# A hybrid attention, recurrence and expert layer on one core: expert weights in 8 KB rows, fetched token rows, and three smaller moves

## The chip, the cores and the metric

The program runs on one core of a Trainium2 chip. A core has TensorE (PE in the profile; its weight loads are PEld), VectorE (DVE), ScalarE (ACT), GpSimd (POOL), SyncE (SP, which here only requests transfers) and 16 DMA engines between HBM and the core's own memory, which has 128 partitions. The metric is the device time of one execution in microseconds, lower is better.

## The reference

Shapes: 512 tokens of latent stream, 256 of context, width 1024, 16 experts of hidden width 1024, float32 throughout.

```python
def block(x, ctx, c, c_ctx, w):
    sh1, sc1, g1, sh2, sc2, g2 = modulation(c, w.ada_w, w.ada_b)      # silu(c) @ ada_w + ada_b
    h     = rmsnorm(x, n1) * (1 + sc1) + sh1
    a     = hgrn_both_directions(h, ctx)                               # gated linear recurrence, 8 heads
    b     = conv3(h)                                                   # short gated depthwise convolution
    o     = attend(h, ctx)                                             # 16 query heads, 4 key heads, head 64
    y     = sig(ga) * (a @ w_pa) + sig(gb) * (b @ w_pb) + sig(gc) * (o @ w_pc)
    x1    = x + g1 * (y @ w_out)
    return rmsnorm(x1 + g2 * experts(rmsnorm(x1, n2) * (1 + sc2) + sh2), fng)

def experts(h, router_w, w_gate, w_up, w_down):        # expert choice: each expert takes 64 of 512 tokens
    aff = softmax(h @ router_w)                        # 512 x 16
    w_sel, idx = top_k(aff.T, 64)
    xs  = h[idx]                                       # 16 x 64 x 1024
    hid = silu(xs @ w_gate) * (xs @ w_up)
    ys  = hid @ w_down * w_sel
    return zeros(512, 1024).at[idx].add(ys)
```

## The kernel before

The stages follow one another. Times are those of the profile's span: recurrence heads and the dense projections to about 540 us, attention to 806, the branch projections with their sigmoid gates to 1130, the output projection with the router's logits to 1190, the choice of tokens to 1215, eight expert pairs to 1661, and a tail to 1697.

**Large products in three passes.** A dense product is made as three passes over split operands (`hH,wh`, `hL,wh`, `hH,wl`, lines L185 to L187): each weight block of 1 MB or 0.5 MB arrives as `raw`, ACT copies it to `wh` (L90) and DVE takes the rest, `wl` (L91). So a block that has landed is of use to PE only when ACT, then DVE, have been over it.

**Attention.** 64 units (query head and quarter of the queries). A unit makes scores (L617, L618, tile `sc`), takes a row maximum on DVE, exponentials on ACT (L623, tile `e`), turns them by six PE transposes (L632, tile `tp`), evicts them half on ACT (L636, tile `pt`) and half on DVE, and multiplies with the values (L647). Scores run two units ahead. Between units a `Filler` issues steps of other dense products (the queries of the next key group, convolution, gate columns), in equal shares per unit. The queries of each group are normalised by a square root on ACT (L582), once for each of two halves; ACT's tables of square root and exponential exclude each other, so each use in the midst of exponentials costs two table loads. Turns of keys and queries (L562, L599) are issued in runs inside those filler steps.

**Branches.** For each of four column blocks, `wblock` requests the gate columns of `w_in`, then two slabs of `ada_w` (`ada_more`, 1 MB each, DVE multiplies each into `acc`, L742), then the projection block `w_p`. When a group of eight slabs is done, `column` turns its sums into a column over partitions: for each of 8 pieces one PE product of a 128x128 piece of `acc` with a single column of ones (L725).

**Experts.** Two experts are worked at a time, 64 tokens each, one in each half of the 128 columns of the stationary operand. Each pair streams 24 weight blocks of 1 MB (gate and up in 4 chunks of 256 channels, then down in 4) through SP's queue, L962, into a ring of 20 slots, plus four slots that hold the first blocks once. `refill` requests a block for each slot that was read. The first 24 requests stand in SP's queue behind the last weights of the output projection, so they go out while that product and the routing run. PE's order in this stage is the order of the code, not a scheduler's: gate and up of pair p (L1099, tiles `pg`, `pu`), then the gather of pair p+1 (L1048: tokens are picked by a product of `x1` with a scaled one-hot matrix `ohs`, 64 PE instructions, evicted by DVE L1053 and ACT L1051 into `xT`), the weights of the chosen tokens (L1062), the scatter of pair p-1 (L1085, L1086, added to `moe` by DVE L1090), the transposes of the hidden values (L1153, after silu on ACT L1139 and the product on DVE L1140), the turned one-hot (L1073, `by_slot`), and down of pair p (L1099, tile `py`). The last pair's down weights are cut into column blocks (`LASTC`), which the tail works one by one, followed by the final norm.

A weight block's layout in `more()`:

```python
wsrc += [mat[e, kk*256:kk*256+256].rearrange("(a p) f -> p a f", p=128) for e in pair]
```

Partition p gets rows p and p+128 of the 256, each a row of 4 KB in HBM.

Of the kernel before, what the change touches and what calls it, by code (L numbers as in the profile page):

```python
# [22 lines left out]
D = 1024  # L23
# [28 lines left out]
def body(tc, x, ctx, cvec, ada_w, ada_b, ada_b0, n1g, n2g, hgn, convw, qg, kg, fng, w_in, w_pa, w_pb, w_pc, w_out,  # L52
# [21 lines left out]
    iota = const.tile([128, 64], F32, name="iota")  # L74
# [96 lines left out]
    last_w = []  # L171

# [372 lines left out]
    def queries(g, w):  # L545
# [10 lines left out]
        qsps[g] = []  # L556
# [8 lines left out]

        for half in range(2):
            p = ps.tile([128, 2, 256], F32, name="d")
            n = 0
            for i in range(2):
                for _ in tok_steps(w, 2 + 2 * half + i, p[:, i]):  # L570
                    yield 1
                    n += 1
                    if half and n % 4 == 0:
                        turn_keys(n // 4 - 1)
                        yield 0.5
            qf = at.tile([128, 2, 4, 64], F32, name="qf")
# [6 lines left out]
            dve.reciprocal(ssq, ssq)  # L583
            dve.tensor_mul(qf, qf, ssq[:, :, :, None].to_broadcast([128, 2, 4, 64]))
# [7 lines left out]
    def turn_queries(g):  # L592
        qst = at.tile([128, 4, S], F32R, name="qst", bufs=2)
        for half, qsp in enumerate(qsps.pop(g)):
            for hp in range(2):
                p = psc.tile([128, 4, 128], F32R, name="tp")
                for h2 in range(2):
                    for t in range(2):
                        pe.transpose(p[:, 2 * h2 + t], qsp[:, t, 2 * hp + h2], identr)  # L599
                act.activation(qst[:, 2 * hp:2 * hp + 2, half * 256:half * 256 + 256],  # L600
                               p.rearrange("p (h t) c -> p h (t c)", t=2).bitcast(F32), AF.Copy)
                yield 0.7
        qsts[g] = qst

    qsps = {}
# [60 lines left out]
    def mixed(c, turn):  # L666

        def steps(w):
            t = turn()
            n = 0  # L670
            for cost in c[1](w):
                yield cost
                n += 1
                if n % 3 == 0:
                    yield next(t, 0.0)
            yield from t
        return c[0], steps
# [3 lines left out]
    Filler([mm0, c2[0], turn0]).drain()  # L681
    fill_items = []
    for g, c in ((1, c2[1]), (2, c2[2]), (3, c3[0])):
        mm, turn = q_items(g)
        fill_items += [mm, mixed(c, turn[1])]
# [5 lines left out]
    with tc.manual_schedule(engines=MANUAL):  # L691
# [4 lines left out]
        for u in range(len(units)):  # L696
            core(turn_probs, u)
            if u + 2 < len(units):
                while units[u + 2][0] not in qsts:
                    fl.fill(1)  # L700
                core(scores, u + 2)
            fl.fill(share / 2)
            while owed:
                owed.pop()()
            if u % 4 == 0 and u:
                core(values, u - 1)
# [15 lines left out]
    def column(src, put):  # L722
        p = pl.tile([128, KC], F32, name="tp")
        for k in range(KC):
            pe.matmul(p[:, k:k + 1], src[:, k * 128:(k + 1) * 128], ones[:, 0:1], start=True, stop=True)  # L725
        put(p)

    def ada_more():
# [14 lines left out]
        if k == KC - 1:  # L743
            lo, hi = accs[g][:, 0:1024], accs[g][:, 1024:2048]
            if g == 1:
                later.append(lambda: gate_rows(lo))
                later.append(lambda: column(hi, lambda p: dve.tensor_copy(ab2[:, 1], p)))
            else:
                later.append(lambda: column(lo, lambda p: dve.scalar_tensor_tensor(ab2[:, 0], p, 1.0, vecs[:, 1],
                                                                                  op0=OP.add, op1=OP.mult)))  # L750
# [25 lines left out]
    def branch(b, w_p, get):  # L776
        hs = ls = None
        for j2 in range(4):
            wg = wblock(w_in, W_GATE + b * 1024 + j2 * 256)
            ada_more()  # L780
            ada_more()
# [8 lines left out]
            wp = wblock(w_p, j2 * 256)  # L790
            for i in range(2):
# [61 lines left out]
    aff = xp.tile([128, 4, NE], F32, name="aff")  # L853
# [17 lines left out]
    def partial_logits(j2, t):  # L871
        tp = pr_.tile([128, 2, 2, 128], F32, name="tp", bufs=2)
        for kk in range(2):
            for i in range(2):
                pe.transpose(tp[:, kk, i], x1[:, t + i, j2 * 256 + kk * 128:j2 * 256 + kk * 128 + 128], ident)
# [32 lines left out]
    dve.reciprocal(ss2, ss2)  # L908
    pl4 = pr_.tile([128, 4, NE], F32, name="tp", bufs=2)
# [22 lines left out]
    wsel = sm.tile([128, NE // 2], F32, name="wsel")  # L932
    slot = sm.tile([128, 4, NE], F32, name="slot")
# [8 lines left out]
    for pr in range(NE // 2):  # L942
        pair = (2 * pr, 2 * pr + 1)
        for kk in range(4):
            for mat in (w_gate, w_up):
                wsrc += [mat[e, kk * 256:kk * 256 + 256].rearrange("(a p) f -> p a f", p=128) for e in pair]
        if pr < NE // 2 - 1:
            for kk in range(4):
                wsrc += [w_down[e, kk * 256:kk * 256 + 256].rearrange("(a p) f -> p a f", p=128) for e in pair]
# [7 lines left out]
    def more(n):  # L957
        for src in wsrc[len(loaded):len(loaded) + n]:
# [3 lines left out]
            sp.dma_start(t, src)  # L962
            loaded.append(t)
# [60 lines left out]
    xs = {}  # L1024
    hot = {}

    def one_hot(pr):
# [6 lines left out]
                          iota[:, None, None, :].to_broadcast(shape), op=OP.is_equal)  # L1034
        ohs = ma.tile([128, 4, 2 * CAP], F32, name="ohs")
        dve.tensor_mul(ohs, ohf, ss2[:, :, None].to_broadcast([128, 4, 2 * CAP]))
        hot[pr] = oh, ohf, ohs

    def gather(pr, k0, p, on_act):

        ohs = hot[pr][2]
        if pr not in xs:
            xs[pr] = ma.tile([128, KC, 2 * CAP], F32, name="xT")
        xT = xs[pr]
        n = p.shape[1]
        for i in range(n):
            for t in range(4):
                pe.matmul(p[:, i], x1[:, t, (k0 + i) * 128:(k0 + i + 1) * 128], ohs[:, t], start=t == 0, stop=t == 3)  # L1048
        for k in range(k0, k0 + n):
            if on_act:  # L1050
# [248 lines left out]
```

## Time and profile before

| | |
|---|---|
| time, median of 3 runs | 1703.13 us (1701.49 to 1704.36) |
| the profiled execution | 1698.42 us, of which its span is 1696.6 us |
| PE busy | 1607.2 us (95% of the span) |
| VectorE, ScalarE, GpSimd busy | 767.9, 527.7, 150.7 us |
| moved by DMA | 305.52 MB, mean 180 GB/s over the span |

The span is the time from the first to the last instruction of the profiled execution. The rows further down are of that one execution.

### The profile page before, as it was taken

How to read it: one execution, taken by the hardware profiler on the slowest of the kernel's cores; microseconds unless marked ns; L12 is line 12 of the kernel's file. 1: busy time of each engine (PE TensorE's matmuls, PEld its weight loads, DVE VectorE, ACT ScalarE, POOL GpSimd, SP SyncE). 2: the span in 40 equal slices, each digit the busy share in tenths (PEclk: the TensorE clock that was granted, in tenths of full speed). 3: DMA queues.
4: the chain of work that ended last, by engine and by line, in shares of the span. 5: the costliest groups of instructions: out<-in, count | busy, mean ns of one | idle time of the engine just before them, and what ended most of it. 6: DMA issues, size and time to landing. Idle time of an engine off the chain costs nothing.

```text
span 1696.6 us, 23600 instructions
## 1 busy us (share of the span) xinstructions
PE 1607.2 (95%) x9896; PEld 1207.7 (71%) x9896; DVE 767.9 (45%) x1173; ACT 527.7 (31%) x934; POOL 150.7 (9%) x142
## 2 busy tenths in 40 slices
PE   6999999999998899899999999999799999999996
PEld 4889898988898788788788888889244344444444
DVE  6364655556545666655646524343411222122124
ACT  4433324334225656654323223233010010011004
POOL 0021212222000000000000100110000000000005
PEclk9999999999999999999999999999899999999998
DMA  9410211122222000100555622348789999999995
GB/s 294 118 41 25 63 38 50 38 75 70 80 80 75 26 25 26 44 33 26 182 191 178 209 85 75 124 148 349 315 320 402 382 409 409 409 409 409 409 395 167
DMA packets 166287, 305.52 MB, mean 180 GB/s; under 512 B 6562, under 2 KB 115618, under 8 KB 164130
## 3 DMA queue, kind: packets, MB, share of 16 engines
q1 hardware_dynamic: 162624, 301.66, 48.9%
q10 hardware_dynamic: 3556, 2.35, 0.4%
q8 instruction: 78, 1.28, 0.3%
q14 instruction: 29, 0.24, 0.0%
HBM read 301.89 MB, written 2.10 MB: 179 GB/s over the span
## 4 chain that ended last, share of the span: by engine, by line
PE 83%; DVE 9%; ACT 5%; issue 2%; POOL 0%; DMA 0%; ACTq 0%; SPq 0%; DVEq 0%; POOLq 0%
PE d L185 14%; PE d L187 14%; PE d L186 14%; PE pg L1099 6%; PE pu L1099 6%; PE py L1099 6%; PE py L1048 3%; PE lv L304 2%; PE tp L647 2%; PE tp L632 2%; DVE wl L91 1%; PE mi L333 1%; PE sc L617 1%; PE sc L618 1%; ACT wh L90 1%
## 5 line engine op out<-in xcount | busy, mean ns | idle before, releaser
L185 PE MATMUL d<-hH,wh 128*128 128x512 f32 x640 | 257.2, 402 | 0.0
L187 PE MATMUL d<-hH,wl 128*128 128x512 f32 x640 | 253.4, 396 | 0.0
L186 PE MATMUL d<-hL,wh 128*128 128x512 f32 x640 | 252.4, 394 | 0.0
L91 DVE TENSOR_TENSOR wl<-raw,wh 128x2048 fp32r<-128x2048 f32 (+1 forms) x78 | 157.8, 2022 | 192.0 <-ACT wh L90 191.8
L90 ACT ACTIVATE wh<-raw 128x2048 fp32r<-128x2048 f32 (+1 forms) x78 | 128.9, 1652 | 218.2 <-PE d L186 167.4
L187 PEld LDWEIGHTS d<-hH,wl 128*128 128x128 f32 x640 | 121.0, 189 | 24.9
L185 PEld LDWEIGHTS d<-hH,wh 128*128 128x128 f32 x640 | 120.8, 189 | 22.3 <-issue 1.6
L186 PEld LDWEIGHTS d<-hL,wh 128*128 128x128 f32 x640 | 121.1, 189 | 21.3 <-issue 0.2
L1099 PE MATMUL pg<-mw,xT 128*64 128x512 f32 x512 | 115.6, 593 | 2.0 <-DVE xT L1053 2.0
L1099 PE MATMUL pu<-mw,xT 128*64 128x512 f32 x512 | 115.3, 592 | 0.0
L1099 PE MATMUL py<-mw,hT 128*64 128x512 f32 x448 | 97.7, 594 | 0.1
L315 POOL TENSOR_TENSOR kk<-kk,tt 128x384 f32<-128x384 f32 x56 | 77.0, 1376 | 190.8 <-DVE tt L317 143.6
L1099 PEld LDWEIGHTS pu<-mw,xT 128*64 128x64 f32 x512 | 36.7, 137 | 73.1 <-issue 72.8
L1099 PEld LDWEIGHTS pg<-mw,xT 128*64 128x64 f32 x512 | 36.1, 137 | 72.2 <-issue 68.8
L185 PE MATMUL d<-wh,hH 128*128 128x256 f32 x288 | 84.1, 292 | 0.0
L187 PE MATMUL d<-wh,hL 128*128 128x256 f32 x288 | 81.7, 284 | 0.0
L186 PE MATMUL d<-wl,hH 128*128 128x256 f32 x288 | 81.6, 283 | 0.0
L1140 DVE TENSOR_TENSOR hid<-hid,pu 128x1024 f32<-128x1024 f32 x8 | 9.8, 1221 | 154.4 <-PE pu L1099 148.0
L187 PE MATMUL d<-brh,wl 128*128 128x512 f32 x192 | 75.6, 396 | 2.6 <-DVE wl L91 2.6
L185 PE MATMUL d<-brh,wh 128*128 128x512 f32 x192 | 75.8, 396 | 1.7 <-ACT wh L90 1.5
L186 PE MATMUL d<-brl,wh 128*128 128x512 f32 x192 | 75.7, 396 | 0.0
L1099 PEld LDWEIGHTS py<-mw,hT 128*64 128x64 f32 x448 | 31.5, 137 | 60.8 <-issue 59.7
(354 smaller groups left out, 2998.1 us busy)
## 6 DMA issues: line engine op xcount, KB each, us to landing
mw<-in_w_gate_dram SPq DMA_DIRECT2D x64, 1024.0 KB, 18.2
mw<-in_w_up_dram SPq DMA_DIRECT2D x64, 1024.0 KB, 18.5
mw<-in_w_down_dram SPq DMA_DIRECT2D x62, 1024.0 KB, 17.4
raw<-in_w_in_dram SPq DMA_DIRECT2D x38, 1024.0 KB, 5.1
raw<-in_ada_w_dram SPq DMA_DIRECT2D x16, 1024.0 KB, 4.9
raw<-in_w_in_dram SPq DMA_DIRECT2D x24, 512.0 KB, 3.8
adaw<-in_ada_w_dram SPq DMA_DIRECT2D x8, 512.0 KB, 8.5
raw<-in_ada_w_dram SPq DMA_DIRECT2D x8, 512.0 KB, 7.8
```

The costliest lines, as they stand in the source:

```text
L90: act.activation(hi, src, AF.Copy)
L91: dve.tensor_sub(lo, src, hi)
L185: pe.matmul(p, lh(k), rh(k), start=k == 0, stop=False)
L186: pe.matmul(p, lh(k), rl(k), start=False, stop=False)
L187: pe.matmul(p, ll(k), rh(k), start=False, stop=k == KC - 1)
L304: pe.matmul(p[:, c], kc[:, c * 128:(c + 1) * 128], q_mix, start=True, stop=True)
L315: pool.tensor_mul(kb[:, :, 1], kb[:, :, 1], tb[:, :, 0, 0:1].to_broadcast([128, n2, m]))
L333: pe.matmul(pv[:, i], kt[:, i], v[:, c], start=True, stop=True)
L632: pe.transpose(tp[:, t], e[:, (t0 + t) * 128:(t0 + t + 1) * 128], ident)
L647: pe.matmul(av[hh * 64:hh * 64 + 64, i], va[:, t, g * 64:g * 64 + 64], pts[hh][:, t], start=t == 0, stop=t == 5)
L1048: pe.matmul(p[:, i], x1[:, t, (k0 + i) * 128:(k0 + i + 1) * 128], ohs[:, t], start=t == 0, stop=t == 3)
L1099: pe.matmul(dst[64 * e:64 * e + 64, hf_], src[:, k, 64 * e:64 * e + 64], wt[e][:, k2, hf_ * 512:hf_ * 512 + 512], start=k == 0, stop=k == ...
```

## The change

1. **8 KB rows.** Gate, up and down blocks (not the last pair's down) are laid out so that partition p gets rows 2p and 2p+1 of the 256, which are 8 KB in one piece. The channel order on partitions thus becomes even, odd. Whatever meets those weights must follow: `every2` takes every second column of `x1`, of the fetched rows and of `hid` as the stationary operand of the products and transposes; the router's rows and the second norm's gain are permuted on the host.
2. **Fetched token rows.** `x1` is stored to HBM (`xd`, four transfers of 512 KB on SP's queue). For pairs 2 to 7 the gather products are gone. The product that finds the chosen tokens' weights gets two more columns, the token's number and its norm factor. GpSimd fetches the 128 rows of 4 KB by an indirect transfer, DVE scales them, and PE turns them by 8 transposes (`turn_rows`). Pairs 0 and 1 still pick by products. The scatter stands behind the transposes of the hidden values now.
3. **A line of turns.** In attention, turns of keys and queries go into a list, `aside`, and are taken one at a time between units. The square root of a query group is taken once for both halves.
4. **Sums by ones.** `column` makes two products of a 128x128 matrix of ones with 512 columns of `acc`, and DVE takes the diagonal by a product with `ident` and a sum over the free axis.
5. **Slabs behind.** The two `ada_w` slabs of a column block are requested behind the projection block `w_p`, not ahead of it.

```diff
@@ queries
+        aside.extend([lambda i=i: turn_keys(i) for i in range(4)])
...
-            ssq = at.tile([128, 2, 4], F32, name="ssq", bufs=2)
-            dve.tensor_reduce(ssq, sq, axis=AX.X, op=OP.add)
-            act.activation(ssq, ssq, AF.Sqrt, scale=1.0 / 64, bias=eps)
+            dve.tensor_reduce(ssq[:, half], sq, axis=AX.X, op=OP.add)
+        act.activation(ssq, ssq, AF.Sqrt, scale=1.0 / 64, bias=eps)
@@ units
-            while owed:
+            if owed:
                 owed.pop()()
+            elif aside:
+                aside.pop(0)()
+                fl.fill(1)
@@ column
-        for k in range(KC):
-            pe.matmul(p[:, k:k + 1], src[:, k * 128:(k + 1) * 128], ones[:, 0:1], start=True, stop=True)
+        for h in range(2):
+            p = ps.tile([128, 512], F32, name="d")
+            pe.matmul(p, ones, src[:, h * 512:(h + 1) * 512], start=True, stop=True)
...
+            dve.tensor_reduce(col[:, 4 * h:4 * h + 4], dg, axis=AX.X, op=OP.add)
@@ branch
             wg = wblock(w_in, W_GATE + b * 1024 + j2 * 256)
-            ada_more()
-            ada_more()
...
             wp = wblock(w_p, j2 * 256)
+            ada_more()
+            ada_more()
@@ experts
+    for t in range(4):
+        sp.dma_start(xd[t * 128:(t + 1) * 128], x1[:, t])
...
-                wsrc += [mat[e, kk * 256:kk * 256 + 256].rearrange("(a p) f -> p a f", p=128) for e in pair]
+                wsrc += [mat[e, kk * 256:kk * 256 + 256].rearrange("(p a) f -> p (a f)", p=128) for e in pair]
...
+    def fetch(pr):
+        xg = mb.tile([128, D], F32, name="hid")
+        pool.indirect_dma_start(xg, None, xd, bass.IndirectOffsetOnAxis(ap=which.pop(pr), axis=0))
+        dve.tensor_scalar(xg, xg, norm[:, pr:pr + 1], None, op0=OP.mult)
+    def turn_rows(pr):
...
+        for k in range(KC):
+            pe.transpose(p[:, k // 4, k % 4], every2(xg, k), ident)
...
+        if 0 < pr and not last:
+            turn_rows(pr + 1)
...
-            gather(pr + 1, 0, pn[:, 0], False)
-            gather(pr + 1, 4, pn[:, 1], True)
-            weights(pr)
-        if not last and waiting:
-            scatter(*waiting, 2, ...)
+        elif pr + 2 < NE // 2:
+            weights(pr + 2)
         hT = ...
+        if not last and waiting:
+            scatter(*waiting, 2, ...)
+        if 0 < pr < NE // 2 - 2:
+            fetch(pr + 2)
```

The line numbers of the changed kernel differ from those of before. Three places of its order follow.

SP's queue at the first branch, before: the slabs `in_ada_w` of a block stand ahead of its projection block `in_w_pc`.

```order
L734 DMA raw<-in_ada_w_dram 128x2048 x2
L176 DMA raw<-in_w_pc_dram 128x8x256
L176 DMA raw<-in_w_in_dram 128x8x256
L734 DMA raw<-in_ada_w_dram 128x2048 x2
L176 DMA raw<-in_w_pc_dram 128x8x256
```

The same place in the changed kernel (L764 is the slab, L181 the dense block).

```order
L181 DMA raw<-in_w_pc_dram 128x8x256
L764 DMA raw<-in_ada_w_dram 128x2048 x2
L181 DMA raw<-in_w_in_dram 128x8x256
L181 DMA raw<-in_w_pc_dram 128x8x256
L764 DMA raw<-in_ada_w_dram 128x2048 x2
```

The projection block has moved ahead of the two slabs in each of the eight column blocks that have slabs.

SP's queue where the experts' first 24 blocks are requested, before: behind the last block of the output projection, from the sixth to the last request.

```order
L962 DMA mw<-in_w_gate_dram 128x2x1024 x2
L962 DMA mw<-in_w_down_dram 128x2x1024
L962 DMA mw<-in_w_up_dram 128x2x1024 x2
L962 DMA mw<-in_w_gate_dram 128x2x1024 x2
L962 DMA mw<-in_w_up_dram 128x2x1024 x2
L962 DMA mw<-in_w_down_dram 128x2x1024 x7
```

The same place in the changed kernel, with the four stores of `x1`.

```order
L1001 DMA mw<-in_w_gate_dram 128x2048
L1001 DMA mw<-in_w_down_dram 128x2048
L941 DMA xd<-x_8639 128x1024 x2
L1001 DMA mw<-in_w_up_dram 128x2048
L941 DMA xd<-x_8639 128x1024 x2
L1001 DMA mw<-in_w_gate_dram 128x2048
L1001 DMA mw<-in_w_up_dram 128x2048
L1001 DMA mw<-in_w_gate_dram 128x2048 x2
L1001 DMA mw<-in_w_up_dram 128x2048 x2
L1001 DMA mw<-in_w_down_dram 128x2048 x7
```

The stores, which need the finished `x1`, stand behind the first ten blocks, and fourteen blocks stand behind the first of them.

PE's queue between gate and up of a middle pair and its down, before (the scatter's row and its partner stand once for eight).

```order
L1099 MATMUL pu<-mw,xT 64x512 x8
L1048 MATMUL py<-ohs,x_8645 128x128 x32
L1062 MATMUL d<-aff,oh 128x16 x4
L1085 MATMUL pg<-hT,ohT 128x512
L1086 MATMUL pg<-yL,ohT 128x512
...
L1153 MATMUL d<-ident,hid 128x128 x8
L1073 MATMUL d<-identr,oh 128x128 x4
L1099 MATMUL py<-mw,hT 64x512 x32
```

The same place in the changed kernel (L1112 turns fetched rows, L1124 finds weights and token numbers, L1226 turns the hidden values, L1151 scatters, L1139 is `by_slot`).

```order
L1165 MATMUL pu<-mw,xT 64x512 x8
L1112 MATMUL py<-ident,hid 128x128 x8
L1124 MATMUL d<-aff,oh 128x18 x4
L1226 MATMUL d<-ident,hid 128x128 x8
L1151 MATMUL pg<-hT,ohT 128x512
L1152 MATMUL pg<-yL,ohT 128x512
...
L1139 MATMUL d<-identr,oh 128x128 x4
L1165 MATMUL py<-mw,hT 64x512 x32
```

The gather's 32 products (64 PE instructions in a trace, since each runs as two) have become 8 transposes, and the transposes of the hidden values stand ahead of the scatter.

## Rows read from the trace of the kernel before

**Rows 1.** The page: PE's busy time, and the DMA engines' share in 40 slices.

```profile
PE 1607.2 (95%) x9896; PEld 1207.7 (71%) x9896; DVE 767.9 (45%) x1173; ACT 527.7 (31%) x934; POOL 150.7 (9%) x142
DMA  9410211122222000100555622348789999999995
```

**Rows 2.** The chain that ended last: share of the span by engine.

```profile
PE 83%; DVE 9%; ACT 5%; issue 2%; POOL 0%; DMA 0%; ACTq 0%; SPq 0%; DVEq 0%; POOLq 0%
```

**Rows 3.** Stretches of the expert stage: start:end, length, busy time per engine, PEclk, DMA share, GB/s.

```profile
1215.00:1277.00 62.00, 58.60 (x326) 28.48 (x328) 6.98 (x18) 5.17 (x9) 0.00 (x0) 1.00 0.81 312
1277.00:1334.00 57.00, 54.89 (x292) 25.77 (x290) 12.02 (x18) 5.63 (x11) 0.00 (x0) 1.00 0.97 384
1334.00:1392.00 58.00, 55.88 (x296) 26.04 (x294) 11.74 (x18) 5.44 (x10) 0.00 (x0) 1.00 1.03 409
...
1564.00:1622.00 58.00, 55.89 (x298) 26.04 (x294) 11.00 (x16) 5.44 (x10) 0.00 (x0) 1.00 1.03 409
```

**Rows 4.** Timeline of PE between up of one pair and its down: start, length, work.

```profile
1419.28 3.84 PE L1048 MATMUL py<-ohs,x 128*128 128x128 f32 x32
1424.57 3.84 PE L1048 MATMUL py<-ohs,x 128*128 128x128 f32 x32 [1.46 <-DVE xT L1053]
1428.25 0.96 PE L1062 MATMUL d<-aff,oh 128*128 128x16 f32 x8
...
1433.69 1.03 PE L1153 MATMUL d<-ident,hid 128*128 128x128 f32 x8
...
1435.43 13.95 PE L1099 MATMUL py<-mw,hT 128*64 128x512 f32 x64
```

**Rows 5.** Line L1099 (all expert products): one of three lines on its waits for weights.

```profile
  DMA mw<-in_w_down_dram: 0.3, 1
```

**Rows 6.** The last weight request, its time to landing; PE's last column block.

```profile
L962 SPq DMA_DIRECT2D mw<-in_w_down_dram x1: 1231/1231/1231, 1664.8 to 1664.8; - x1
...
DMA to landing us min/median/max: 6.5/6.5/6.5
...
1680.49 1.97 PE L1194 MATMUL pg<-mw,hT 128*64 128x128 f32 x32
```

**Rows 7.** Timeline of DVE and ACT in the same pair as group 4.

```profile
1419.49 1.22 DVE L1140 TENSOR_TENSOR hid<-hid,pu 128x1024 f32<-128x1024 f32 x1 [24.74 <-PE pu L1099]
...
1415.99 1.02 ACT L1139 ACTIVATE hid<-pg 128x1024 f32<-128x1024 f32 x1 [21.96 <-PE pg L1099]
```

**Rows 8.** Stretches in which slabs of `ada_w`, 8 KB rows, move alone.

```profile
862.00:864.50 2.50, 2.50 (x12) 2.06 (x11) 0.00 (x0) 0.00 (x0) 0.00 (x0) 1.00 0.85 344
894.00:896.50 2.50, 2.50 (x13) 2.07 (x12) 1.85 (x3) 1.78 (x3) 0.00 (x0) 1.00 0.87 354
```

**Rows 9.** The page: transfers of 512 KB of `x` on ACT's queue, us to landing.

```profile
xr<-in_x_dram ACTq DMA_DIRECT2D x4, 512.0 KB, 12.0
```

**Rows 10.** Timeline of PE: eight products whose moving operand alternates single elements, then pairs.

```profile
308.51 1.49 PE L304 MATMUL lv<-qq,kc 128*128 128x128 f32 x8
312.36 1.12 PE L304 MATMUL lv<-qq,kc 128*128 128x128 f32 x8
```

**Rows 11.** Attention: what PE waited for in 546 to 727 us; ACT's groups in 540 to 806.

```profile
PE tp L632 <- ACT pt L636: 11.5, 7, 3.1
...
L623 ACT ACT_TABLE_LOAD x7 | 9.0, 1283 | 4.4 <-DVE mx L621 4.4
L582 ACT ACT_TABLE_LOAD x6 | 7.7, 1283 | 0.1
```

**Rows 12.** Start of the first branch: DVE and PE in the timeline, and a stretch.

```profile
813.60 2.35 DVE L742 SCALAR_TENSOR_TENSOR acc<-raw,sc,acc 128x2048 f32<-128x2048 f32 x1
...
821.21 0.79 PE L187 MATMUL d<-brh,wl 128*128 128x512 f32 x1 [2.58 <-DVE wl L91]
...
819.90:826.70 6.80, 5.49 (x13) 4.33 (x14) 3.64 (x3) 1.91 (x1) 0.00 (x0) 0.50 0.52 176
```

**Rows 13.** PE's groups in 990 to 1130 us: the single-column products.

```profile
L725 PE MATMUL tp<-ones,acc 128*128 128x1 f32 x31 | 3.6, 250 | 0.0
```

More of the change, by code (lines that the diff above doesn't have):

```diff
@@ L571, in queries @@
                     yield 1
[L572 to L576, printed above, removed]
+            qf = at.tile([128, 2, 4, 64], F32, name="qf", bufs=2)
+            qfs.append(qf)
             act.activation(qf.rearrange("p t h d -> p t (h d)"), p, AF.Copy)
@@ L593, in turn_queries, with turn @@
         qst = at.tile([128, 4, S], F32R, name="qst", bufs=2)
[L594 to L605, printed above, removed]
+        def turn(half, hp):
+            p = psc.tile([128, 4, 128], F32R, name="tp")
+            for h2 in range(2):
+                for t in range(2):
+                    pe.transpose(p[:, 2 * h2 + t], qsps[g][half][:, t, 2 * hp + h2], identr)
+            act.activation(qst[:, 2 * hp:2 * hp + 2, half * 256:half * 256 + 256],
+                           p.rearrange("p (h t) c -> p h (t c)", t=2).bitcast(F32), AF.Copy)
+            if half and hp:
+                qsts[g] = qst
+        aside.extend([lambda i=i: turn(i // 2, i % 2) for i in range(4)])
+        return iter(())
+    qsps, aside = {}, []
     units = [(g, hp, qt, hh) for g in range(4) for hp in range(2) for qt in range(4) for hh in range(2)]
@@ L664, in q_items, with early_part, later_part @@
         return (W_AQ + g * 256, lambda w: queries(g, w)), (None, lambda: turn_queries(g))
[L666 to L677, printed above, removed]
+    parts = []
+    def early_part(c, w):
+        it = c[1](w)
+        parts.append(it)
+        for _ in range(KC):
+            yield next(it)
+    def later_part():
+        yield from parts.pop()
     c2, c3 = conv_items(2, at, "u", 1), conv_items(3, at, "u", 1)
     mm0, turn0 = q_items(0)
-    Filler([mm0, c2[0], turn0]).drain()
+    first = Filler([mm0, c2[0], turn0])
+    first.fill(33)
+    for _ in range(4):
+        first.fill(4)
+        aside.pop(0)()
+    first.drain()
+    for _ in range(4):
+        aside.pop(0)()
     fill_items = []
@@ L1023, in body @@
     pm, pm_e = opn("pm", space=PSUM, bufs=1)
-    xs = {}
-    hot = {}
+    xs, hot, which, fetched = {}, {}, {}, {}
     def one_hot(pr):
@@ L1103, in early @@
     def early(k0):
-        gather(0, k0, ps.tile([128, 2, 128], F32, name="d"), False)
+        pick(0, k0, ps.tile([128, 2, 128], F32, name="d"), False)
     with tc.manual_schedule(engines={mybir.EngineType.DVE}):
         one_hot(0)
+        scaled(0)
         early(0)
+    turned = {}
     waiting = None
@@ L1140, in body @@
         dve.tensor_mul(hid, hid, pu.rearrange("p a b -> p (a b)"))
-        if not last:
+        if pr == 0:
+            scaled(1)
             pn = pm.tile([128, 2, 4, 128], F32, name="py")
-            gather(pr + 1, 0, pn[:, 0], False)
-            gather(pr + 1, 4, pn[:, 1], True)
-            weights(pr)
-        if not last and waiting:
-            scatter(*waiting, 2, lambda t: pm.tile([128, 2, 512], F32, name=("pg", "pu")[t // 2]))
+            pick(1, 0, pn[:, 0], False)
+            pick(1, 4, pn[:, 1], True)
+            weights(0)
+            weights(1)
+        elif pr + 2 < NE // 2:
+            weights(pr + 2)
         hT = mb.tile([128, KC, 128], F32, name="hT")
@@ L1152, in body @@
                 k = 4 * h4 + i
-                pe.transpose(tp[:, i], hid[:, k * 128:(k + 1) * 128], ident)
+                pe.transpose(tp[:, i], (hid[:, k * 128:(k + 1) * 128] if last else every2(hid, k)), ident)
             act.activation(hT[:, 4 * h4:4 * h4 + 4], tp, AF.Copy)
-        if 0 < pr < NE // 2 - 1:
-            oT_t = by_slot(pr)
-            if pr + 2 < NE // 2:
-                one_hot(pr + 2)
+        if not last and waiting:
+            scatter(*waiting, 2, lambda t: pm.tile([128, 2, 512], F32, name=("pg", "pu")[t // 2]))
+            turned[pr + 1] = by_slot(pr + 1)
+            if pr + 3 < NE // 2:
+                one_hot(pr + 3)
         py = pm.tile([128, 2, 512], F32, name="py")
@@ L1168, in body @@
             acc = mc.tile([128, 4, D], F32, name="moe")
-            oT_t = by_slot(0)
+            for i in range(2):
+                turned[i] = by_slot(i)
             one_hot(2)
+            one_hot(3)
         yt = mb.tile([128, D], F32, name="hid")
```

114 lines of the change are left out of this document (77 added, 37 removed).

## The prediction

> **What bounds the kernel now.** The page comes first: PE is busy for 1607.2 us, 95% of the span [rows 1], and the chain that ended last is 83% PE and 0% DMA [rows 2]. So PE's own instructions set the time nearly everywhere, and what PE is spared counts, unless something else is close behind. In the last third something is: the DMA slices stand at 9 there [rows 1]. The stretches of the expert stage tell it closely. From the third pair on the DMA share is 1.03 at 409 GB/s, and five such stretches of 57 or 58 us look alike [rows 3]. A pair takes PE those 57.5 us. It needs 24 blocks of 1 MiB, 25.17 MB, and at 409 GB/s that is 61.5 us. The transfers are already 4.0 us per pair slower than PE. PE does not feel it, since it never waited more than 0.3 us for any weight block [rows 5]: it lives on blocks requested before the stage began. How much of that store is left at the end is read from three rows: the last request went out at 1664.8 and landed 6.5 us later, at 1671.3; PE began its last column block at 1680.5 [rows 6]. Weights are 9.2 us early at the end, and no more.
>
> **The experts' stage: PE's side.** Before, PE's gap between up and down runs from 1419.28 to 1435.43, 16.15 us [rows 4]. Of this the gather is 3.84 + 1.46 (waiting for DVE's eviction) + 3.84, the weights 0.96; the scatter with its waits lies between 1429.1 and 1433.7, 4.6 us, and the turned one-hot takes 0.5. After, the gather's 64 instructions become 8 transposes, about 1.1 us (the hidden values' eight take 1.03 [rows 4]). But the hidden values are wanted earlier. Silu takes 1.02 us on ACT, the product 1.22 us on DVE [rows 7], and in the new order they no longer lie under the gather. DVE has one eviction and four small copies ahead of the product, about 1 us. Counted from the end of up: turns 1.1, weights 0.96, then the product ends at about 3.7, and some 2 us of PE wait remain. The gap is 1.1 + 0.96 + 2 + 1.03 + 4.6 + 0.5 = 10.2 us: 6 us less. For six pairs PE would have 36 us less to do (bounds: 30, if the wait is 3 us, to 40, without it).
>
> **The same stage: the transfers' side.** A store of 9.2 us cannot cover 36 us. From about the fourth pair on PE must wait for weights, and the end is set by the transfers: their last landing, then what followed in before. So the gain is 9.2 us, less whatever the transfers end later by.
> - 8 KB rows. While the slabs of `ada_w` move, which have rows of 8 KB, the share is 0.85 for 344 GB/s and 0.87 for 354 [rows 8]: 405 and 407 GB/s per full share. The expert blocks with 4 KB rows make 409 at 1.03, 397 [rows 3]. The ratio of 0.978 over the 345 us from 1277 to 1622 [rows 3] gives -7.6, with the blocks behind them about -8 us. Bounds: 0, if a full queue moves both alike, and -16, twice the ratio.
> - Fetched rows: six times 128 rows of 4 KB, 3.15 MB, at 409 to 419 GB/s: +7.6 us in the same queues.
> - The store of `x1`, 2.1 MB or 5 us, stands in SP's queue with fourteen of the first 24 blocks behind it, and so these wait until `x1` is done. In 1215 to 1277 the share is 0.81 against 1.03 later [rows 3]: 13 idle us, which cover it. If that cover were gone, +5.
> - Strided stationary operands. No row of before shows one. The nearest: eight products whose moving operand alternates between two streams element by element take 1.49 us, against 1.12 with pairs [rows 10], 0.05 us each. By this the 112 picks of pair 0's stage and some transposes cost +6 us before the transfers take over, and by nothing different, 0. The new operand steps through one stream only, and weight loads overlap: +3.
>
> Together -8 + 7.6 + 3 = +2.6, and the gain is 9.2 - 2.6 = **6.6 us** (bounds -9, a loss, with no help of rows, no cover and full strides, to +18).
>
> The Trainium skill speaks against the strides: "Advanced Engine Details and Errata", Memory Cachelines, says that any non-contiguous access pattern slows matmuls significantly, and that two consecutive elements should be contiguous. The trace agrees in sign for a moving operand, by 33% [rows 10]; no run here shows a stationary one. By the rule the +3 would be +6, and the sum 3 us worse.
>
> **Attention.** PE waited 11.5 us, seven times, for ACT's eviction of turned probabilities; ACT loaded tables 7 + 6 times, 1.283 us each [rows 11]. With one square root per group instead of two these become 3 + 4, so 3 of 7 such waits go: -4.9 us. Turns taken singly leave PE fewer runs that hold up a unit's eviction, perhaps -2. Against it: the filler's shares are larger and one more step goes with each turn, so by the order it runs out some eleven units before the end. Those units have little but their own path (maximum, exponential, turn, eviction) for PE to wait on; the work that stood between them now stands earlier, and there it fills holes only where there are some. +3, from 0 to +16. Sum **-4** (bounds -12 to +9).
>
> **Branch start.** At 813.60 DVE starts the product with a slab, 2.35 us, while the split operands of the first projection wait behind it; PE then waits 2.58 us for `wl`, after 1.5 us for `wh`, and the clock falls to 0.50, 1.2 of 2.4 GHz, from 819.9 to 826.7 [rows 12]. Requested behind the projection block, slabs are later than that block and DVE's order changes. 4.1 us of gaps and up to 3.4 us (half of 6.8) lie there: **-5.5** (bounds -7.5 to -2, since DVE now makes all the splits). Later blocks don't matter: PE is full there.
>
> **Columns and logits.** 31 instructions of single-column products take 3.6 us [rows 13]. There are 48 (three columns of eight pieces, two passes each), so 5.6. After, there are six products of 512 columns, twelve passes at 13.95 / 64 = 0.22 us, as in the expert products [rows 4]: 2.6. But their results pass two DVE steps before use, and what PE is spared is partly waited for: **-1** (-3 to +1). The logits' 32 strided transposes: **+1** (0 to +1.7, by the 0.05 us above).
>
> **Sum.** -6.6 - 4 - 5.5 - 1 + 1 = -16.1: 1698.4 becomes 1682.3 for a profiled execution. The median of before is 0.28% above its profiled execution, and by this ratio the prediction is 1687 us.
>
> **Rivals.**
> - *Rows bring nothing.* The queues are full at 1.03 either way, and 409 GB/s may be all there is. For it: the slabs' rows come from stretches that are not full. Then the transfers end 8 us later: 1695 us. The skill's "DMA: Bandwidth & Descriptors", Where 436 GB/s comes from, names about 358 GB/s as a core's limit for HBM, and no row size would help; 409 [rows 3] is above it, and the measurement decides. Chance 0.15.
> - *Transfers don't bind.* If fetches and rows fit beside each other, with PE freeing blocks earlier so that the 0.97 of 1277 to 1334 [rows 3] also becomes 1.03 (3 us) and rows at twice the ratio (8 us), the end is 11 us earlier, and attention at its good bound gives 8: 1668 us. Against it: the share is at its top. Chance 0.13.
> - *Attention's end starves.* The fillers are gone, and each of eleven units waits about 1 us: attention +7 instead of -4, 1698 us. Chance 0.11.
> - *Slower: 8 KB rows move worse in a full queue.* Place: SP's 144 blocks after the first forty. Under 409 GB/s each per cent costs 3.5 us of those 345, and the 8 us of gain are lost as well. It decides where (16.1 - 8) / 3.5 = 2.3% are lost, at about 400 GB/s; at 385, 6% less, the time is 1687 + 8 + 21 = 1716. For it: longer packets hold an engine longer, so fetched 4 KB rows and weights could block each other. Against it: slabs show no such thing [rows 8], and a 512 KB transfer on another queue took only 12.0 us beside full traffic [rows 9], while a fetch has gate and up of one pair, 57.5 - 16.15 - 13.95 = 27.4 us [rows 3, 4], until its rows are turned. Chance 0.11.
>
> **How the numbers follow.** The forecast's own case has 0.50, with 1679 to 1695. A change under 0.2%, 3.4 us, can't be told from none. Faster: 0.50 + 0.13, nearly all of rows-bring-nothing (1695, 0.14) and half of starved attention (0.06): 0.83. Same: the rest of these two, 0.06. Slower: 0.11. The range 1668 to 1702 takes in the first three rivals and leaves out the slower one and the tails.
>
> **What would show it.** Right: from the fourth pair on, L1165's wait lines name `mw` transfers with over 15 us in all; GB/s of the stage at 415 or more with share unchanged; gaps of about 10 us between up and down; three table loads at the square root; no half clock at the first branch. Wrong: GB/s still 409; PE waiting for `hid<-xd`, or DVE's scaling; waits at L638 in attention's last units; the half clock still there. The forecast falls if rows of 8 KB are no faster and attention gives nothing, for then little is left but the branch start.

## The result

The changed kernel takes 1674.26 us in the median of 4 runs, against 1702.77 us before: a ratio of 0.983 (0.9812 to 0.9847), 28.5 us less. The two profiled executions differ less: spans of 1673.9 and 1696.6 us, 22.7 us apart. The profiled execution of before, 1698.42 us, lies 4.4 us under its median, that of the changed kernel, 1675.70, lies 1.4 us over its own. What follows is worked out on spans, and ratios are compared with ratios.

### The profile page after: what moved, and what is told of

It is laid out like the page before. It is cut to its first block, busy times and chain, and to the rows that moved or that the text cites. A ratio compares the mean times of both kernels' runs of the same rounds, so it can differ in the third digit from the quotient of the medians.

```text
span 1673.9 us, 22891 instructions
## 1 busy us (share of the span) xinstructions
PE 1576.4 (94%) x9524; PEld 1170.2 (70%) x9524; DVE 775.2 (46%) x1193; ACT 520.4 (31%) x924; POOL 157.6 (9%) x150
## 4 chain that ended last, share of the span: by engine, by line
PE 50%; DMA 8%; DVE 5%; ACT 3%; issue 1%; ACTq 0%; DVEq 0%; SPq 0%
PE d L190 8%; PE d L192 8%; PE d L191 8%; DMA mw<-in_w_up_dram 5%; PE pg L1165 5%; PE pu L1165 5%; PE py L1165 4%; DMA mw<-in_w_down_dram 2%; PE tp L653 2%; PE tp L638 2%; PE sc L623 1%; PE sc L624 1%; DVE wl L91 1%; ACT wh L90 1%; PE d L1040 1%
## 5 line engine op out<-in xcount | busy, mean ns | idle before, releaser
L1165 PE MATMUL pu<-mw,xT 128*64 128x512 f32 x512 | 121.9, 594 | 8.6 <-DMA mw<-in_w_up_dram 8.6
L1165 PE MATMUL pg<-mw,xT 128*64 128x512 f32 x512 | 121.1, 595 | 8.2 <-DMA mw<-in_w_gate_dram 6.2
L629 ACT ACTIVATE e<-sc,mx 128x768 f32<-128x768 f32 x64 | 57.7, 901 | 42.0 <-DVE mx L627 41.7
```

The source lines that it names most:

```text
L629: act.activation(e, pf, AF.Exp, bias=mx, accum_out=dens[g, hp][:, qt, hh:hh + 1])
L1165: pe.matmul(dst[64 * e:64 * e + 64, hf_], src[:, k, 64 * e:64 * e + 64], wt[e][:, k2, hf_ * 512:hf_ * 512 + 512], start=k == 0, stop=k == ...
```

## The profile after

The page: busy times, the DMA share in 40 slices, and the chain that ended last. These answer to [rows 1, 2].

```profile
PE 1576.4 (94%) x9524; PEld 1170.2 (70%) x9524; DVE 775.2 (46%) x1193; ACT 520.4 (31%) x924; POOL 157.6 (9%) x150
DMA  9320112022222011011365533346989999999996
...
PE 50%; DMA 8%; DVE 5%; ACT 3%; issue 1%; ACTq 0%; DVEq 0%; SPq 0%
```

PE is busy for 31 us less, and the chain, which had no DMA before, now has 8% (its shares add up to 67% of the span here and to 99% before, so it is a hint and no more). So PE was relieved, and something else took its place in part. Stretches of the expert stage tell where (start:end, length, busy time per engine, PEclk, DMA share, GB/s), to be read beside [rows 3].

```profile
1264.00:1317.00 53.00, 50.27 (x247) 20.75 (x247) 13.24 (x25) 6.67 (x12) 1.15 (x1) 1.00 0.98 402
1317.00:1370.00 53.00, 50.35 (x238) 20.82 (x236) 12.07 (x19) 5.67 (x10) 0.94 (x1) 0.97 1.01 420
1370.00:1422.00 52.00, 49.37 (x239) 19.75 (x236) 12.00 (x19) 5.67 (x10) 0.94 (x1) 1.00 1.01 419
1422.00:1474.00 52.00, 49.37 (x238) 19.88 (x236) 11.99 (x19) 5.67 (x10) 0.94 (x1) 1.00 1.01 419
1474.00:1535.00 61.00, 51.19 (x238) 20.56 (x236) 11.98 (x19) 5.66 (x10) 0.94 (x1) 1.00 1.01 419
1535.00:1599.00 64.00, 53.15 (x232) 21.39 (x230) 11.62 (x15) 5.66 (x10) 0.94 (x1) 0.97 1.01 420
```

Each stretch is one pair, from the second to the seventh of eight. Four pairs take 52 to 53 us, where they took 57.5. Then the sixth and the seventh take 61 and 64 us with the same work: 9 and 12 us more. The data rate is 419 GB/s at a share of 1.01. The list of PE's waits from 1190 us on (us in total, times, longest) names what the two long pairs wait for, and a new wait beside it.

```profile
PE d L1226 <- DVE hid L1211: 13.3, 7, 2.4
PE pu L1165 <- DMA mw<-in_w_up_dram: 8.6, 6, 1.9
PE pg L1165 <- DMA mw<-in_w_gate_dram: 6.2, 5, 1.3
```

PE waits for weights for 14.8 us in this list (matmuls alone), and for the hidden values for 13.3 us, of which 1.8 us, the last pair's, is no more than its wait was before. The gap of one pair, in PE's timeline and, last, ACT's, shows the second wait in its place.

```profile
1398.26 1.22 PE L1112 MATMUL py<-ident,hid 128*128 128x128 f32 x8
1399.32 0.96 PE L1124 MATMUL d<-aff,oh 128*128 128x18 f32 x8
1402.08 1.22 PE L1226 MATMUL d<-ident,hid 128*128 128x128 f32 x8 [1.80 <-DVE hid L1211]
1408.34 0.53 PE L1139 MATMUL d<-identr,oh 128*128 128x128 f32 x4 [0.45 <-ACT hT L1227]
...
1399.57 1.02 ACT L1210 ACTIVATE hid<-pg 128x1024 f32<-128x1024 f32 x1 [26.55 <-PE py L1112]
```

The gap between up and down is 1408.8 - 1398.3 = 10.5 us, where it was 16.15 [rows 4]. Silu starts at 1399.57, and what released it is not the gate's product but the turn of the fetched rows, L1112: they lie in the memory that the hidden values will take. In the kernel before silu began 3.3 us ahead of the end of up (1415.99 against 1419.28, [rows 4, 7]).

The first expert product stands in a row of each kernel, before and after (first and last start).

```profile
L1099 PE MATMUL pg<-mw,xT x512: 592/592/643, 1215.3 to 1657.2; 128*64 128x512 f32 x171
```

```profile
L1165 PE MATMUL pg<-mw,xT x512: 592/592/644, 1201.1 to 1633.1; 128*64 128x512 f32 x171
```

The stage with its tail, from there to the end, takes 481.3 and 472.8 us: 8.5 less. The other 14.2 us were gained ahead of it. How the 8.5 us came about is read as [rows 6] was: the last weight request, its time to landing, and PE's last column block.

```profile
L1001 SPq DMA_DIRECT2D mw<-in_w_down_dram x1: 1596/1596/1596, 1648.2 to 1648.2; - x1
...
DMA to landing us min/median/max: 6.9/6.9/6.9
...
1657.84 1.97 PE L1273 MATMUL pg<-mw,hT 128*64 128x128 f32 x32
```

The last weights land at 1655.1, 454.0 us after the first expert product, where it was 456.0: the transfers end 2.0 us earlier. PE comes to that block 2.7 us later, where it was 9.2: of the store of weights, 6.5 us were used up. Together that is the 8.5 us.

In attention's time, 540 to 850 us, PE's waits are these, and last stand ACT's table loads at the square root, in 540 to 806 us:

```profile
PE tp L638 <- ACT pt L642: 6.2, 6, 2.4
PE sc L623 <- ACT qst L603: 3.1, 1, 3.1
PE tp L638 <- ACT e L629: 2.5, 1, 2.5
PE d L192 <- DVE wl L91: 0.9, 1, 0.9
...
L584 ACT ACT_TABLE_LOAD x3 | 3.8, 1283 | 0.1
```

The waits for evictions on ACT are 6.2 us instead of 11.5 [rows 11]; the 1.5 and 2.6 us at the first branch [rows 12] are gone, with 0.9 us at a later block in their place. The square root has three table loads instead of six. Three stretches: attention's start, its end, and the first branch.

```profile
544.00:555.00 11.00, 7.78 (x38) 6.73 (x36) 5.27 (x9) 6.57 (x14) 0.00 (x0) 0.53 0.29 95
...
797.00:808.00 11.00, 11.00 (x92) 9.08 (x91) 6.92 (x13) 7.19 (x12) 0.00 (x0) 1.00 0.15 49
808.00:850.00 42.00, 41.06 (x182) 33.68 (x181) 25.40 (x18) 10.87 (x10) 0.00 (x0) 1.00 0.54 188
```

PE is full after attention's last scores, and the clock stays at 1.00 (2.4 GHz) at the branch. But at attention's start it is half, 1.2 GHz, for most of 11 us: worse than before, where the stretch from 541 to 552 us has a mean of 0.84, and not forecast.

## The experiments

All ratios are against the kernel before, run on the same chip beside them; the changed kernel's is 0.983 (0.9812 to 0.9847). Differences in us are 0.1% = 1.7 us of these ratios, or those of spans where said.

A time read from the one profiled execution of a kernel can be off, and kernels with the same code show by how much. The first expert product stands at 1197.9 to 1201.7 us in five kernels that have the same code up to there (the changed one, and those with fewer pairs fetched or rows turned early), so 3 us there say little. The stage with its tail takes 471.3 to 472.8 us in five kernels with the changed kernel's stage. Attention, from its first scores to the first branch product, is steadier: 264.7 to 265.0 us in eight kernels, 266.2 in a ninth that has 3.4 us at half clock in it.

**The experts' change, two by two.** Three kernels complete the table.

```diff
 4 KB rows, fetch kept:
-                wsrc += [mat[e, ...].rearrange("(p a) f -> p (a f)", p=128) for e in pair]
+                wsrc += [mat[e, ...].rearrange("(a p) f -> p a f", p=128) for e in pair]
...
-        return v[:, o:o + 255:2]
+        return v[:, k * 128:k * 128 + 128]
 8 KB rows, no fetch:
-            turn_rows(pr + 1)
...
-            fetch(pr + 2)
...
+            scaled(pr + 1)
+            pick(pr + 1, 0, pn[:, 0], False)
+            pick(pr + 1, 4, pn[:, 1], True)
```

> The changed kernel with expert blocks in 4 KB rows again and all operands contiguous; rows are still fetched. Theory (transfers pace the later pairs, and the two parts are worth something only together): the stage moves at 409 instead of 419 GB/s, so some 375 us of blocks take 2.5% longer, +9 us: about 1683 us, and waits of the expert products for weights rise from 15 to some 24 us. Rival A (fetching alone gives the gain, rows nothing): 1674 us and waits as they are. Rival B (strides cost PE more than rows give): under 1674 us.

> The changed kernel with 8 KB rows, but no fetch and no store of x1: pairs 2 to 7 pick by products as pairs 0 and 1 do. Theory (PE paces, if it must pick): a pair takes 57 to 58 us again, PE waits for no weights, and the expert stage with its tail takes 481 us as before, not 473: about 1682 us. Rival A (rows alone give the gain, the fetch only adds 3.1 MB of traffic): 1667 us, for 7.6 us of traffic less. Rival B (fetch gives its full 6 us for each of 6 pairs, transfers don't matter): 1710 us.

> The changed kernel with neither part of the experts' change: 4 KB rows, contiguous operands, all pairs picked by products. With the other three runs it gives a table of two by two. Theory (rows alone bring nothing while PE paces): 1686 to 1688 us, as with 8 KB rows and no fetch (1687.5), less some 5 us for the contiguous operands at most. Rival (rows help even then): 1692 us or more.

| ratio to before | picked by products | fetched |
|---|---|---|
| 4 KB rows, contiguous | 0.9888 (0.9873 to 0.9904) | 0.9872 (0.9850 to 0.9895) |
| 8 KB rows, strided | 0.9912 (0.9895 to 0.9930) | 0.9830 (0.9812 to 0.9847) |

Fetching alone gives 0.16%, 2.7 us, within the intervals; 8 KB rows alone lose 0.24%, 4 us, with intervals that still overlap; both give 0.58%, 10 us. So the 8 KB rows, worth nothing or less while PE sets the pace, bring 7 us once the token rows are fetched, clear of the intervals. The theory of the transfers' pace stands; both its rivals (one part gives all) fall. With fetches and 4 KB rows PE waits 18.9 us for weights instead of 14.8; some 24 were expected. The kernel with 8 KB rows and no fetch came out 5.5 us above the value expected of it: a pair takes 58.4 us there, 57.9 with contiguous operands, and 57.5 in the kernel before, whose gap has another order. With 8 KB rows and no fetch PE waits for weights in this line alone (expert products, that kernel):

```profile
  DMA mw<-in_w_down_dram: 1.1, 4
```

and the price of the strides shows in its timeline, beside the kernel with neither:

```profile
1410.76 4.04 PE L1094 MATMUL py<-ohs,x 128*128 128x128 f32 x32
1416.26 4.04 PE L1094 MATMUL py<-ohs,x 128*128 128x128 f32 x32 [1.46 <-DVE xT L1086]
```

```profile
1407.12 3.84 PE L1093 MATMUL py<-ohs,x 128*128 128x128 f32 x32
1412.42 3.84 PE L1093 MATMUL py<-ohs,x 128*128 128x128 f32 x32 [1.46 <-DVE xT L1085]
```

A stationary operand with a stride of two costs 0.2 us in 32 instructions, 6 ns each. Eight transposes of fetched rows, 1.22 us in the changed kernel, take less with 4 KB rows and contiguous operands; the stride costs 16 ns each there:

```profile
1396.02 1.09 PE L1111 MATMUL py<-ident,hid 128*128 128x128 f32 x8
```

The rate of the stage stands in one stretch of each kernel, 4 KB rows fetched, then the changed kernel:

```profile
1420.00:1620.00 200.00, 172.09 (x772) 67.16 (x770) 43.37 (x65) 18.22 (x32) 2.82 (x3) 0.99 1.03 409
```

```profile
1420.00:1600.00 180.00, 156.72 (x718) 62.90 (x716) 36.01 (x54) 16.99 (x30) 2.81 (x3) 0.99 1.01 419
```

**Fewer pairs fetched.** `fetch` for pairs 2 to 5, or 2 to 4, and products for the rest.

```diff
-        if 0 < pr < NE // 2 - 2:
+        if 0 < pr and pr + 2 in FETCH:
             fetch(pr + 2)
```

> The changed kernel with pairs 2 to 5 fetched and pairs 6 and 7 picked by products again. Theory (the last pairs wait for weights, 9 and 12 us longer than the others): the two gathers, 12 us of PE, lie under those waits, and 1.05 MB less of traffic ends 2.5 us earlier: about 1672 us, with weight waits of about 4 us. Rival (PE's path sets the time even there): +12 us, 1686 us.

> The changed kernel with only pairs 2 to 4 fetched, 5 to 7 picked by products. Theory: 18 us more for PE against 21 us of waiting in the last pairs, and 1.6 MB less of traffic, 3.8 us: between 1670 and 1674 us, with nearly no wait for weights left, since PE and transfers then end together. Rival (PE's path sets the time even there): 1692 us.

0.9840 (0.9822 to 0.9858) and 0.9838 (0.9818 to 0.9858): the same as the changed kernel. 12 and 18 us of gathers disappeared under the waits, and the rival falls. But the smaller traffic gave nothing either: a miss. With PE fuller, the waits for weights are 4.4 and 1.5 us, so PE paces again. The fetches' traffic and the gathers they save seem to balance; neither was measured by itself.

**Rows turned earlier.** The eight transposes go ahead of the last quarter of gate and up, their evictions stay behind silu; then the same with pairs 2 to 4 fetched.

```diff
+            if kk == 3 and 0 < pr and pr + 1 in FETCH:
+                pt_ = turn_rows(pr + 1)
...
-            turn_rows(pr + 1)
         hid = mb.tile([128, D], F32, name="hid")
```

> The changed kernel with the fetched rows turned ahead of the last quarter of gate and up instead of behind it, so that silu, whose tile takes the place of the fetched rows, need not wait for the turn. Theory (silu waits for that place): PE's waits for the hidden values fall from 13.3 us to under 4, gaps of a pair shrink by 2 us and the half-clock stretches in gaps vanish; but the transfers pace the end, so only the part before they take over may show: 1670 to 1673 us. Rival (silu is late for another reason): waits unchanged, 1673 us.

> The changed kernel with rows turned ahead of the last quarter of gate and up, and only pairs 2 to 4 fetched, 5 to 7 picked by products. Theory (PE and transfers end together once the waits for the hidden values are gone, and 1.6 MB less of traffic ends 3.8 us earlier): 1668 to 1671 us. Rival (the transfers' end sets the time less than PE's last pair): 1671 to 1675 us.

0.9818 (0.9803 to 0.9834) and 0.9833 (0.9820 to 0.9847): a gain of 2 us at most, not clear of the intervals, and none in the second, where the theory wanted 3 to 6 us and the time lies in its rival's range. The first kernel's rows show ACT's silu, DVE's product, PE's wait, and its list of waits.

```profile
1394.67 1.02 ACT L1215 ACTIVATE hid<-pg 128x1024 f32<-128x1024 f32 x1 [23.31 <-PE pg L1169]
...
1398.12 1.22 DVE L1216 TENSOR_TENSOR hid<-hid,pu 128x1024 f32<-128x1024 f32 x1 [15.98 <-PE pu L1169]
...
1399.40 1.50 PE L1239 MATMUL d<-ident,hid 128*128 128x128 f32 x8 [0.42 <-DVE hid L1216]
...
PE d L1239 <- DVE hid L1216: 5.6, 7, 1.8
```

Silu is released by the gate's product again, and the wait falls from 1.80 to 0.42 us, 13.3 to 5.6 in sum (under 4 was expected). This does not single out the memory place, for in the changed kernel DVE was late too:

```profile
1400.46 0.31 DVE L1131 COPY wsel<-d 64x1 f32<-64x1 f32 x2
1400.80 1.22 DVE L1211 TENSOR_TENSOR hid<-hid,pu 128x1024 f32<-128x1024 f32 x1
```

Silu ends there at 1400.59, but DVE has small copies until 1400.77, so an earlier silu alone would not have brought the product forward. It is so in five of the six gaps; in the sixth, without these copies, silu ends last. With rows turned early both are moved: silu comes earlier, and DVE takes the product ahead of the copies. Which of the two was worth how much stays open.

What PE wins there it seems to wait for later. The second to the fifth pair take 208.8 us, against 210.2 in the changed kernel and 213.7 in the kernel with the square root per half (below), which has the changed kernel's stage. From there to the end it is 199.2, 199.4 and 194.5 us, and the whole stage takes 471.1, 472.8 and 471.4.

**The first branch.** Slabs ahead of the projection block again.

```diff
             wg = wblock(w_in, W_GATE + b * 1024 + j2 * 256)
+            ada_more()
+            ada_more()
```

> The changed kernel with the slabs requested ahead of the projection block, as before. Theory (the slab's product on DVE holds up the first projection's operands and the clock falls): gaps of 1.5 and 2.6 us and a half-clock stretch return at the first branch, +7 us: 1680 us against 1673. Rival (the gap went because attention now ends earlier, and the order of requests does nothing): 1673 us, with no gap there.

0.9878 (0.9860 to 0.9895): +8 us; the first expert product comes 7.0 us later (1208.1), more than the scatter of 3.8 us. The rival falls. The wait stands in this kernel's list, and the clock in a stretch:

```profile
PE d L190 <- ACT wh L90: 5.2, 1, 5.2
...
813.00:820.00 7.00, 6.49 (x15) 4.65 (x16) 4.52 (x2) 2.11 (x2) 0.00 (x0) 0.51 0.50 171
```

**Attention.** All of the old turns; then only the square root taken for each half.

```diff
             dve.tensor_reduce(ssq[:, half], sq, axis=AX.X, op=OP.add)
+            act.activation(ssq[:, half], ssq[:, half], AF.Sqrt, scale=1.0 / 64, bias=eps)
-        act.activation(ssq, ssq, AF.Sqrt, scale=1.0 / 64, bias=eps)
```

> The changed kernel with attention's turns, square roots and filler steps as before. Theory (they are worth what the traces show between the start of attention and the first branch, 7.3 us): 1680 us. Rival (part of it came from elsewhere, such as a shorter leftover of fillers): 1675 to 1677 us.

> The changed kernel with the line of turns kept, but the square root taken for each half of a query group again: three square roots and three table loads back to exponentials more, 7.7 us of ACT. Theory A (the table loads cause attention's waits): +4 us, 1677 us, and PE's waits for evictions rise from 6 to 11 us. Theory B (runs of turns caused them): 1673 us, waits unchanged.

Old turns: 0.9908 (0.9891 to 0.9926), 13 us more, where 7 were expected. In its profiled execution, the fastest of five, 8.7 us have come by the first branch product (817.3 against 808.6) and 8.5 by the first expert product (1209.6). The rest of the median's 13 us goes with the clock: the runs of 1683.2 and 1684.0 us have a mean granted clock of 0.983, those of 1687.4 and 1687.5 have 0.981, and that of 1689.5 has 0.979; a mean lower by 0.002 over 1685 us is 3.4 us. Where the clock fell in them no trace shows.

The square root per half: 0.9844 (0.9829 to 0.9860), 2.4 us more, which the intervals do not tell from none. The trace does: first scores and first branch product in the changed kernel, then in this one, which loads tables six times at the square root again.

```profile
543.69 0.50 PE L623 MATMUL sc<-kst,qst 128*128 128x512 f32 x1 [3.14 <-ACT qst L603]
...
808.60 0.39 PE L190 MATMUL d<-brh,wh 128*128 128x512 f32 x1
```

```profile
544.19 0.50 PE L623 MATMUL sc<-kst,qst 128*128 128x512 f32 x1 [3.13 <-ACT qst L603]
...
812.64 0.39 PE L190 MATMUL d<-brh,wh 128*128 128x512 f32 x1
```

264.9 us became 268.4: 3.5 us more, where eight kernels agree within 0.3. The waits for evictions in the kernel with old turns, then in the one with the square root per half:

```profile
PE tp L637 <- ACT pt L641: 11.6, 7, 3.1
```

```profile
PE tp L638 <- ACT pt L642: 9.3, 8, 2.4
```

So the table loads make 3.1 of 5.4 us of these waits, and the rest comes with the old turns and filler steps, which were put back together: each theory has a part.

**Columns.** Single-column products again.

```diff
+        for k in range(KC):
...
+            pe.matmul(p[:, k:k + 1], piece, ones[:, 0:1], start=True, stop=True)
```

> The changed kernel with the sums of the slabs turned into columns by 48 single-column instructions again (for the two permuted columns by strided pieces). Theory (PE takes as long either way, 4.2 us for the last two columns, but behind the single-column products the clock falls for 3.4 us): +1.7 us, 1675 to 1676 us, and the half-clock stretch near 985 us is back. Rival (DVE's two steps cost as much as the clock): 1673 us.

0.9860 (0.9843 to 0.9876), 5 us more by the ratio, with intervals that just overlap. In the trace 1.95 us have come by the end of the branches, near the 1.7 expected, with the clock falling again:

```profile
980.00:990.00 10.00, 10.00 (x36) 8.12 (x37) 3.06 (x3) 0.60 (x1) 0.00 (x0) 0.76 0.33 105
```

The changed kernel takes six of the eight passes for the last two columns in 3.0 us, 0.5 each, so PE itself was spared nothing there:

```profile
978.13 3.00 PE L747 MATMUL d<-acc,ones 128*128 128x512 f32 x6
```

**Attention's start.** Rows turned early, and the first queries' turns taken between steps of the convolution.

```diff
-    first = Filler([mm0, c2[0], turn0])
-    first.fill(33)
-    for _ in range(4):
-        first.fill(4)
+    first = Filler([mm0, turn0, c2[0]])
+    first.fill(35)
+    for _ in range(8):
+        first.fill(3.8)
         aside.pop(0)()
     first.drain()
-    for _ in range(4):
-        aside.pop(0)()
```

> The changed kernel with rows turned early, as in the run before, and with the first queries' turns taken between steps of the first convolution, not behind it. Theory (attention starts 3 us later than before because four turns and their evictions stand alone, and the clock falls there for 10.2 us): the wait of 3.1 us goes and the half-clock stretch shrinks, 1667 to 1669 us. Rival (the wait only moves ahead to the turns, whose operands are not ready): 1671 us.

0.9804 (0.9791 to 0.9818), 1668.31 us in the median, 2.4 us by the ratios under the kernel with rows turned early alone, with intervals that overlap. The first expert product comes at 1193.6, 7.5 us before the changed kernel's and 4.3 before the earliest of the five. No half clock is left at attention's start:

```profile
530.00:560.00 30.00, 26.77 (x184) 23.44 (x184) 21.11 (x30) 19.87 (x40) 3.63 (x4) 1.00 0.22 70
```

This is the fastest version of all; its interval overlaps the changed kernel's slightly.

## Why the prediction was right, and by how much

The direction and the mechanism were right and 1674.3 us lies in the range, 12.7 us under the value given. 6.6 us of these lie between the sum, -16.1, and the difference of the spans, -22.7; the rest is the scatter of the profiled executions about their medians. By its terms:

- *Transfers bind once PE is spared.* Right: a pair took 52 to 53 us (forecast 51.5) until the weights ran short, in the sixth pair and not from about the fourth. The stage gave 8.5 us, forecast 6.6, and the two-by-two table shows that it takes both parts. Its two pieces differ from the sum's: 6.5 of the 9.2 us of store were used, and the transfers ended 2.0 us earlier, not 2.6 later.
- *8 KB rows, -8.* Right: 419 against 409 GB/s. Going back costs 0.42%, 7 us, with what the strides cost already taken off.
- *Strides, +3.* Near, by luck: pair 0 takes 0.7 us more than with contiguous operands (63.2 against 62.5 from its first gate product to the next pair's), and the gaps of the four pairs behind it 0.3 each (10.5 against 10.2, where the clock does not fall), some 2 us in all. The mixed moving operand [rows 10] was a poor neighbour: 0.05 us each there, 0.006 in products and 0.016 in transposes here. The Trainium skill's rule ("Advanced Engine Details and Errata", Memory Cachelines), that non-contiguous patterns slow matmuls significantly, stands there under PSUM, the memory of TensorE's results, while this stationary operand lies in SBUF, the core's main memory. Here a stride costs 5% in products and 12% in transposes.
- *Fetched rows, +7.6 of traffic.* Not told apart: with less of it PE became the bound. A fetch landed in 8.6 us in the median, against the 12.0 taken as a neighbour [rows 9], far inside its cover. The store of `x1` was covered, as argued, as far as the first pairs show no wait for weights.
- *PE's wait for the hidden values, 2 us.* Right, in size (1.80) and in the cause named: one eviction and four small copies lie ahead of DVE's product, which ends 3.8 us after the end of up (forecast 3.7). What the prediction had left out, the memory place that silu shares with the fetched rows, comes to the same moment within 0.2 us.
- *Attention, -4.* Undersized. From the kernel before to the changed one the first branch product, less the wait ahead of it, came 7.3 us earlier, and the old turns give 7.4 back by the end of the branches. Attention itself gave 10.3 (275.2 to 264.9 us), though it started 3.0 us later (543.7 against 540.7); other kernels with this start have 541.7 to 545.6. Table loads were worth some 3.5, not 4.9; turns and filler steps gave the rest, some 7 and not 2; and the +3 for a starved end did not come: PE is full there. That rival fell.
- *Branch start, -5.5.* Undersized: 7.0 in the trace and 8 by the ratio, about the better bound.
- *Columns, -1.* The size was off, 2, and the mechanism wrong: a pass was taken at 0.22 us and took 0.5, so the instructions cost as much as before. What went was the half clock behind them.
- *Logits, +1.* Not told from nothing: from the branches' last product to the first expert product it is 84.4 us before and 84.9 after, and 84.4 to 85.9 in the other kernels.

Ahead of the stage the terms measured, 7.3, 7.0 and 2, come to 16 us, where 14.2 were found; the difference is no more than the scatter of the first expert product.

## What to carry to other kernels

When one resource is at 95% and the next at its own limit, count the store between them: here 9.2 us of weights ahead at the end bounded what some 34 us less work for PE (5.6 in each of six gaps) could give, and two parts that are worth 3 and -4 us alone were worth 10 together. Ask which memory place a prefetched tile shares: its reader then delays whoever writes there next. And before one late input of a wait is taken for its cause, look when the other inputs were ready: here two ended within 0.2 us of each other. A short wait of PE costs its length and sometimes a stretch at half clock behind it, but closing it pays only where PE sets the pace.

## What the hardware showed that was not expected

In the changed kernel the clock fell for 3.4 us in three of the gaps where PE waits 1.8 to 2.4 us for the hidden values (0.97 in 1317 to 1370), and in others not. In the kernel with rows turned early, whose waits there are 0.4 us, it stays at its upper level (a mean of 1.00 over 1264 to 1500). But short waits do not always keep it up: in the kernel with attention's start changed, which has the same early turn, it falls for 3.4 us in a gap with waits of 0.3 us for weights and 0.74 us for the hidden values:

```profile
1440.00:1450.00 10.00, 9.23 (x40) 5.76 (x36) 4.97 (x11) 1.83 (x4) 0.00 (x0) 0.83 1.01 417
```

In this stage such stretches hardly show in the time, since the transfers set the end: the kernel with the slabs ahead has six of them between 1300 and 1590 us, the changed kernel two, and their stages take 471.3 and 472.8 us. Elsewhere they do, as the five runs with old turns suggest.
